# Four units with seven products in nearly every gate and up block of the two FFNs

## The chip, the core and the metric

The kernel runs on one core of a Trainium2 chip. Times are device microseconds (us) of one execution; "before" is the median of three runs. The profile is one further execution, taken by the hardware profiler, and its own time is given beside its span below. The engines are named as in the profile: PE (TensorE, matrix products), PEld (its weight loads), DVE (VectorE), ACT (ScalarE), POOL (GpSimd) and SP (whose queue issues most of the loads).

## The reference, cut to what matters

One decoder layer in float32: a SwiGLU half-step, a mixer with two gated linear recurrences, and a second SwiGLU half-step, each between two RMS norms. The change lies in the first two products of the two SwiGLU steps:

```python
def swiglu(x, w_gate, w_up, w_down):
    return (jax.nn.silu(x @ w_gate) * (x @ w_up)) @ w_down

f1 = swiglu(rms_norm(h, ffn1_pre_norm[l]), ffn1_w_gate[l], ffn1_w_up[l], ffn1_w_down[l])
h = h + 0.5 * rms_norm(f1, ffn1_post_norm[l])
# ... the mixer ...
f2 = swiglu(rms_norm(h, ffn2_pre_norm[l]), ffn2_w_gate[l], ffn2_w_up[l], ffn2_w_down[l])
```

`x` is 256 x 2048 and the gate and up weights are 2048 x 5504, so each weight is read once and used for two row tiles of 128.

## The kernel before

**Blocks.** Each FFN walks over the 5504 columns of gate and up in eleven blocks, `j = 0` to `10`: first a narrow one of 384 columns, then ten wide ones of 512. `gemm_pair` computes one block of gate and the same block of up together, for both row tiles: four sums, held in four PSUM tiles `c` (`c00`, `c01`, `c10`, `c11`: row tile, then gate or up). The inner dimension of 2048 is cut into eight units of 256. In the second FFN the narrow block goes through `gemm_block` instead, which is what `begin` being None stands for.

**A plain unit.** Every float32 number is split into two float32r parts, high and low, and a product is three matmuls: high by high (L159), low x by high w (L160), high x by low w (L161). ACT makes the high part `whi` of a weight tile (L153) and DVE the low part `wlo` by a subtraction (L155). A plain unit has two such 128x1024 chunks, one of gate and one of up, and eight products, which is 24 matmuls of 128x512.

**A unit with seven products.** `seven` does the same unit as a 2x2 block product by a scheme of the Strassen kind: sums of the four weight tiles are formed first, and then seven products are enough, which is 21 matmuls. DVE forms the sums (`wsum` 128x1024, `raw` 128x512, `wsum` 128x512, all at L245) and three low parts (two `wlo` of 128x1024 and `wsuml` of 128x1536, also L245). ACT makes four high parts (L280, L282, L284, L286), and the tiles arrive in four loads of 256 KB (L274 to L277) where a plain unit has two of 512 KB (L135). The low part `wsuml` comes last; its first reader on PE is the third matmul of the product `p5`, which is the first L161 matmul that reads `wsuml` in each such unit. The sums of `x` that these products need are made once per FFN (`operand_sums`).

**How many.** `SUMS` has three units with seven products (2, 4, 6), `FOUR` has four (2, 4, 5, 6). Where a block has four, the steps are set so that one plain chunk stands between two units with seven products:

```python
if late:
    at = range(6, 6 + 2 * len(sevens), 2)
elif len(sevens) > len(SUMS):
    at = range(3, 3 + 2 * len(sevens), 2)
else:
    at = [2 * u - j for j, u in enumerate(sevens)]
```

Before, blocks of odd `j` have four and wide blocks of even `j` three, in both FFNs. The last wide block is `j = 10`.

**The end of a block.** The first two chunks of the next block are split ahead (`following`). DVE adds the parts `psum` of the shared products (`share`), closes the four `c` tiles (L245, `c<-c,psum`), and multiplies by ACT's silu (L705). ACT then rearranges the two results (`halves`, L709), its queue issues two DMA transposes (L713), and some steps later it writes the turned rows to `hT` (L718). All of these stand in the in-order streams of DVE and ACT among the next block's splits.

**Buffers.** `raw`, `whi` and `wlo` have rings of five tiles, the row tiles (`wsum`, `wsumh`, `wsuml`, `psum`) a ring of three, and PSUM has eight tiles.

Of the kernel before, what the change touches and what calls it, by code (L numbers as in the profile page):

```python
# [33 lines left out]
SUMS = (2, 4, 6)  # L34
FOUR = (2, 4, 5, 6)
# [53 lines left out]
def kernel(ctx: ExitStack, tc: tile.TileContext, a: dict, out: bass.AP):  # L89
# [15 lines left out]
    def nm(s):  # L105
        uid[0] += 1
        return f"{s}_{uid[0]}"
# [55 lines left out]
    def gemm_block(w_dram, c0, w, lhs, nkt=KT, held=None, raws=(), ready=()):  # L163

        raws, ready = list(raws), list(ready)
        nb = -(-w // CB)
        step = 2 // nb  # L170
        pss = [[ps_tile(f"mm{t}") for _ in range(nb)] for t in range(NT)]

        def chunk(k0, alloc):
            if ready:
                return ready.pop(0)
            raw = raws.pop(0) if raws else None
            src = w_dram[k0 * P:(k0 + step) * P, c0:c0 + w]
            return wchunk(src.rearrange("(k p) c -> p k c", p=P) if nb == 1 else
                          src.rearrange("p (n c) -> p n c", n=nb), w // nb, alloc, raw)

        def mm(t, k0, parts):
            for i, part in enumerate(parts):
                kt = k0 + i % step
                mm3(pss[t][i // step][:, :w // nb], lhs(t, kt), part, kt == 0, kt == nkt - 1)

        if held is None:
            for k0 in range(0, nkt, step):
                parts = chunk(k0, ring_alloc)
                for t in range(NT):
                    mm(t, k0, parts)  # L190
                side.pump()
        else:
            kept = []
            for i, k0 in enumerate(range(0, nkt, 2)):
                kept.append((k0, chunk(k0, ring_alloc if i < RING else held)))
                mm(0, *kept[-1])
                side.pump()
            for k in kept:
                mm(1, *k)
                side.pump()  # L200
            side.flush()
        return pss if nb > 1 else [ps[0] for ps in pss]
# [122 lines left out]
    def first_of(w_dram, c0, w=CB):  # L325
        def chunk(i):
            return wchunk(w_dram[2 * i * P:2 * (i + 1) * P, c0:c0 + w]
                          .rearrange("(k p) c -> p k c", p=P), w)
        return chunk

    def gemm_pair(ws, w, lhs, sums, ready=(), following=(), raws=(), sevens=SUMS,
                  late=False):

        raws = list(raws)
        nu = KT // 2

        b = Blocks(lambda i, kt: ws[i][0][kt * P:(kt + 1) * P, ws[i][1]:ws[i][1] + w],  # L340
                   w, lhs, part_of(sums))

        def split(i, k0):
            return wchunk(None, w, raw=raws.pop(0)) if raws else first_of(*ws[i], w)(k0 // 2)

        steps = [(u, i) for u in range(nu) if u not in sevens for i in range(2)]
# [6 lines that stand above are left out]
        for j, u in zip(at, sevens):  # L355
            steps.insert(j, (u, None))
        ready = list(ready)
        for j, (u, i) in enumerate(steps):
            side.fast = late
            if any(i is None for _, i in steps[j:j + 2]):  # L360
                side.full = True
            if i is None:
                b.seven(u, u == sevens[-1])
                continue
            k0 = 2 * u
            parts = ready.pop(0) if ready else split(i, k0)
            if (u, i) == (nu - 1, 0) and sevens:
                ready = [split(1, k0)]
                b.share()
            for t in range(NT):  # L370
                b.plain((k0, k0 + 1), t, i, parts, u == nu - 1)
            side.pump()
        ready = [chunk(0) for chunk in following]
        for i in range(2 if sevens else 0):
            for t in range(NT):
                b.close(t, i)
        side.full = side.fast = False
        return *[[b.c[t][i] for t in range(NT)] for i in range(2)], ready
# [298 lines left out]
    def ffn(pre, x, rs, post, pre_next, begin=None, ready=(), then=None):  # L677
        with ExitStack() as fctx:
# [8 lines left out]
            def x_sums():  # L687
                return operand_sums(
                    x, lambda i: tiles4(new_part(i).rearrange("p i c -> p (i c)")), sums)

            raws = begin(x_sums) if begin else ()
# [9 lines left out]
            blocks = [FIRST] + list(range(0, FIRST, CB))  # L701

            def finish(t, f0, w, u, s):
# [13 lines left out]
                src = turned[:, :2 * n, :].rearrange("p (h j) k -> p h j k", h=2)  # L717
                nc.scalar.activation(dst.rearrange("p j (k h) -> p h j k", h=2), src, AF.Copy)  # L718

            for j, f0 in enumerate(blocks):  # L720
                w = min(CB, DFF - f0)
                following = [first_of(a[pre + s], f1) for f1 in blocks[j + 1:j + 2]
                             for s in ("_w_gate", "_w_up")]
                if j or begin:
                    g, u, ready = gemm_pair(
                        [(a[pre + "_w_gate"], f0), (a[pre + "_w_up"], f0)], w, xl, sums, ready,
                        following, () if j else raws, (FOUR if j % 2 else SUMS) if j else ())
                else:
                    g = gemm_block(a[pre + "_w_gate"], f0, w, xl, held=held, ready=ready)
                    ready = ()  # L730
                s = []
                for t in range(NT):
                    st = fwork.tile([P, CB], F32, tag="silu", name=nm("silu"))
                    nc.scalar.activation(st[:, :w], g[t][:, :w], AF.Silu, scale=rs[t])
                    s.append(st)
                if not (j or begin):
                    side.spawn(x_sums())
                    u = gemm_block(a[pre + "_w_up"], f0, w, xl)
                hT[f0 // CB] = fpool.tile([P, 4, NT * P], F32, tag="hT", name=nm("hT"), bufs=11)
                for t in range(NT):  # L740
                    side.spawn(finish(t, f0, w, u[t], s[t]))
# [537 lines left out]
    def begin(x_sums):  # L1279

        raws = []

        def load_h(*tns):
            for t, n in tns:
                nc.sync.dma_start(h[t][n], a["x"][t * P:(t + 1) * P, n * CB:(n + 1) * CB])

        def load_w(*ics):
            for i, c in ics:
                raws.append(wload(a[("ffn1_w_gate", "ffn1_w_up")[i]]
                                  [2 * c * P:2 * (c + 1) * P, FIRST:]  # L1290
                                  .rearrange("(k p) c -> p k c", p=P), DFF - FIRST,
                                  apart=not (i or c)))

        load_h((0, 0))
        load_w((0, 0))
        load_h((1, 0))
        load_w((1, 0), (0, 1))
        load_h((0, 1))
        load_w((1, 1))
        load_h((1, 1))  # L1300
        load_w((0, 2))
        load_h((0, 2), (1, 2), (0, 3), (1, 3))

        idle = work.tile([P, CB], F32R, tag="tmp", name="idle", bufs=3)
        nc.gpsimd.memset(idle.bitcast(F32), 0.0)
        ps = ps_tile()

        def idling(n):
            for _ in range(n):
                nc.tensor.matmul(ps, lhsT=idle[:, :P], rhs=idle, start=True, stop=True)  # L1310

        idling(9)
        tp = ps_tile()
        nc.tensor.transpose(tp[:, :KT], wrow, ident[:KT, :KT])
        first_ops.append(nc.vector.tensor_copy(wcol, tp[:, :KT]))
        side.spawn(first_norm(x, rs, idling, x_sums))
        return raws

    x, rs, ready = ffn("ffn1", x, rs, "ffn1_post_norm", wcols[:, 1, :], begin,
                       then=first_of(a["w_in"], O_GQ))  # L1320
    x, rs, ready = mixer(x, rs, ready, first_of(a["ffn2_w_gate"], FIRST, DFF - FIRST))
    ffn("ffn2", x, rs, "ffn2_post_norm", None, ready=ready)
    side.flush()

# [45 lines left out]
```

## Time and profile before

| | |
|---|---|
| median of 3 runs | 2064.32 us (2063.22 to 2066.75) |
| the profiled execution, its own time | 2066.25 us |
| its span in the profile | 2064.3 us |
| PE busy | 2051.2 us (99%) |
| DVE busy | 1858.0 us (90%) |
| ACT busy | 1304.9 us (63%) |

The span is what the profile shows from the first to the last instruction; the execution's own time is 1.95 us longer. Busy time counts an instruction from its start to its end, and consecutive instructions overlap a little on PE, DVE and ACT. In the rows of the timeline the first number is the start in us from the span's start, the second the duration (of all of them, where `x2` or more stand together), and a bracket gives the engine's idle time before the row and what ended it.

### The profile page before, as it was taken

What the parts mean: (1) busy time and instruction counts of PE and PEld (TensorE: products, weight loads), DVE (VectorE), ACT (ScalarE), POOL (GpSimd) and SP (SyncE); (2) the same over time, 40 slices, a digit from 0 to 9 for tenths busy, and PEclk for the clock granted to TensorE, in tenths of its full rate; (3) what the DMA queues carried; (4) which work ended last, traced back from release to release, by engine and by line L of the source; (5) the groups of instructions that cost most, each with busy time, mean ns of one, the idle gap of its engine ahead of it and who ended that gap; (6) DMA issues with size and microseconds to landing.
All of it is one profiled execution on the core that took longest, in us unless ns stands there. A gap on an engine that the chain in (4) does not pass through costs nothing. (4 is left out here: it accounts for less than half of the span.)

```text
span 2064.3 us, 28994 instructions
## 1 busy us (share of the span) xinstructions
PE 2051.2 (99%) x10337; PEld 1702.9 (82%) x10337; DVE 1858.0 (90%) x2187; ACT 1304.9 (63%) x1714; POOL 41.1 (2%) x87
## 2 busy tenths in 40 slices
PE   9999999999999999999999999999999999999998
PEld 9888888888888888878888888888888888888886
DVE  7999999998999779989999897578999999999996
ACT  7666666666666576577655554465666666766663
POOL 1000000000000100000000000010000000000000
PEclk9999999999999999999999999999999999999999
DMA  8767677676767467556565566747767767776663
GB/s 261 215 208 241 196 220 218 209 227 207 226 196 230 148 198 222 162 174 192 169 203 188 181 223 214 218 157 200 234 193 218 227 210 215 219 235 200 213 206 133
DMA packets 246105, 423.50 MB, mean 205 GB/s; under 512 B 63476, under 2 KB 71863, under 8 KB 245960
## 3 DMA queue, kind: packets, MB, share of 16 engines
q1 hardware_dynamic: 194896, 401.80, 61.7%
q10 hardware_dynamic: 51064, 19.84, 4.8%
q8 instruction: 81, 1.33, 0.3%
q14 instruction: 64, 0.52, 0.1%
HBM read 406.11 MB, written 4.19 MB: 199 GB/s over the span
## 5 line engine op out<-in xcount | busy, mean ns | idle before, releaser
L155 DVE TENSOR_TENSOR wlo<-raw,whi 128x1024 fp32r<-128x1024 f32 (+3 forms) x498 | 582.8, 1184 | 70.9 <-ACT whi L153 70.0
L153 ACT ACTIVATE whi<-raw 128x1024 fp32r<-128x1024 f32 (+3 forms) x498 | 504.8, 1026 | 217.5 <-PE c L160 74.0
L159 PE MATMUL c<-whi,xhi 128*128 128x512 f32 (+1 forms) x1270 | 494.5, 390 | 0.0
L161 PE MATMUL c<-wlo,xhi 128*128 128x512 f32 (+1 forms) x1270 | 491.5, 387 | 0.0
L160 PE MATMUL c<-whi,xlo 128*128 128x512 f32 (+1 forms) x1270 | 491.3, 387 | 0.0
L245 DVE TENSOR_TENSOR wlo<-raw,whi 128x1024 fp32r<-128x1024 f32 x252 | 299.4, 1218 | 36.9 <-ACT whi L284 23.6
L161 PEld LDWEIGHTS c<-wlo,xhi 128*128 128x128 f32 x1270 | 238.4, 188 | 47.9 <-DVE wlo L245 0.8
L159 PEld LDWEIGHTS c<-whi,xhi 128*128 128x128 f32 x1270 | 238.4, 188 | 47.4 <-ACT xhi L471 0.6
L160 PEld LDWEIGHTS c<-whi,xlo 128*128 128x128 f32 x1270 | 238.5, 188 | 46.2
L284 ACT ACTIVATE whi<-raw 128x1024 fp32r<-128x1024 f32 x126 | 133.1, 1057 | 201.2 <-DVE raw L245 95.0
L245 DVE TENSOR_TENSOR wsuml<-wsum,wsumh 128x1536 fp32r<-128x1536 f32 x126 | 220.6, 1751 | 8.0 <-ACT wsumh L286 8.0
L160 PE MATMUL c<-whi,hklo 128*128 128x512 f32 x558 | 217.2, 389 | 0.3 <-DVE hklo L155 0.3
L161 PE MATMUL c<-wlo,hkhi 128*128 128x512 f32 x558 | 217.2, 389 | 0.1
L159 PE MATMUL c<-whi,hkhi 128*128 128x512 f32 x558 | 217.2, 389 | 0.0
L282 ACT ACTIVATE wsumh<-wsum 128x1024 fp32r<-128x1024 f32 x126 | 132.6, 1053 | 92.7 <-DVE wsum L245 70.7
L280 ACT ACTIVATE whi<-raw 128x1024 fp32r<-128x1024 f32 x126 | 132.4, 1051 | 60.8 <-PE c L160 49.4
L245 DVE TENSOR_TENSOR wsum<-raw,raw 128x1024 f32<-128x1024 f32 x126 | 153.4, 1218 | 18.2 <-DMA raw<-in_ffn_w_down_dram 15.7
L160 PEld LDWEIGHTS c<-whi,hklo 128*128 128x128 f32 x558 | 104.7, 188 | 22.3 <-DVE hklo L155 0.6
L161 PEld LDWEIGHTS c<-wlo,hkhi 128*128 128x128 f32 x558 | 104.7, 188 | 22.2 <-DVE wlo L245 0.5
L159 PEld LDWEIGHTS c<-whi,hkhi 128*128 128x128 f32 x558 | 104.7, 188 | 21.8
L245 DVE TENSOR_TENSOR c<-c,psum 128x512 f32<-128x512 f32 x135 | 87.4, 690 | 11.5 <-PE c L161 11.2
L245 DVE TENSOR_TENSOR wsum<-raw 128x512 f32<-128x512 f32 x126 | 87.0, 690 | 3.6
(346 smaller groups left out, 3153.4 us busy)
## 6 DMA issues: line engine op xcount, KB each, us to landing
raw<-in_ffn_w_down_dram SPq DMA_DIRECT2D x124, 512.0 KB, 4.7
raw<-in_w_in_dram SPq DMA_DIRECT2D x104, 512.0 KB, 4.5
raw<-in_ffn_w_gate_dram SPq DMA_DIRECT2D x90, 512.0 KB, 4.6
raw<-in_ffn_w_up_dram SPq DMA_DIRECT2D x90, 512.0 KB, 4.4
raw<-in_ffn_w_gate_dram SPq DMA_DIRECT2D x140, 256.0 KB, 4.0
raw<-in_ffn_w_up_dram SPq DMA_DIRECT2D x140, 256.0 KB, 3.9
raw<-in_w_in_dram SPq DMA_DIRECT2D x128, 256.0 KB, 3.6
raw<-in_ffn_w_down_dram SPq DMA_DIRECT2D x96, 256.0 KB, 3.7
```

What stands on the lines that cost most here:

```text
L153: last[0] = nc.scalar.activation(hi, src, AF.Copy)
L155: nc.vector.tensor_tensor(lo, src, hi.bitcast(F32), op=ALU.subtract)
L159: nc.tensor.matmul(ps, lhsT=xhi, rhs=whi, start=start, stop=False)
L160: nc.tensor.matmul(ps, lhsT=xlo, rhs=whi, start=False, stop=False)
L161: nc.tensor.matmul(ps, lhsT=xhi, rhs=wlo, start=False, stop=stop)
L245: return nc.vector.tensor_tensor(o, x, y, op=op)
L280: nc.scalar.activation(ahi, ra, AF.Copy)
L282: nc.scalar.activation(hi[:, 0:2, :], wsum[:, 0:2, :], AF.Copy)
L284: nc.scalar.activation(bhi, rb, AF.Copy)
```

## The change

A new function chooses the units of a block. In the first FFN `begin` is set, and blocks 1 to 9 have four units with seven products. In the second FFN blocks 2 to 9 have four, and block 1 has three. Block 10 keeps three in both.

```diff
+            def sevens_of(j):
+                if not j:
+                    return ()
+                return FOUR if j < len(blocks) - 1 and (begin or j > 1) else SUMS
+
             for j, f0 in enumerate(blocks):
...
                 if j or begin:
                     g, u, ready = gemm_pair(
                         [(a[pre + "_w_gate"], f0), (a[pre + "_w_up"], f0)], w, xl, sums, ready,
-                        following, () if j else raws, (FOUR if j % 2 else SUMS) if j else ())
+                        following, () if j else raws, sevens_of(j))
```

So blocks 2, 4, 6 and 8 of each FFN go from three such units to four, and block 1 of the second FFN from four to three: seven units more in all, and 21 matmuls fewer.

The order of instructions moves at the seams between blocks. DVE in the first FFN, from the last multiplication by silu of block 3 to the first `wsuml` of block 4, before (block 4 has three units; the first two rows are the two plain chunks that come ahead of its first unit with seven products):

```order
L705 SCALAR_TENSOR_TENSOR silu_1659<-c_265_1312,r_421,silu_1659 128x512
L155 TENSOR_TENSOR wlo_1703<-raw_1700,whi_1702 128x1024
L155 TENSOR_TENSOR wlo_1721<-raw_1718,whi_1720 128x1024
L245 TENSOR_TENSOR wsum_1738<-raw_1736,raw_1737 128x1024
L245 TENSOR_TENSOR raw_1737<-wsum_1738,raw_1736 128x512
L245 TENSOR_TENSOR wsum_1738<-raw_1737 128x512
L245 TENSOR_TENSOR wlo_1746<-raw_1736,whi_1745 128x1024
L245 TENSOR_TENSOR wlo_1748<-raw_1737,whi_1747 128x1024
L245 TENSOR_TENSOR wsuml_1740<-wsum_1738,wsumh_1739 128x1536
```

And DVE at such a seam now (blocks 4 and 5 of the first FFN, both with four units):

```order
L705 SCALAR_TENSOR_TENSOR silu_2022<-c_345_1675,r_421,silu_2022 128x512
L155 TENSOR_TENSOR wlo_2066<-raw_2063,whi_2065 128x1024
L245 TENSOR_TENSOR wsum_2083<-raw_2081,raw_2082 128x1024
L245 TENSOR_TENSOR raw_2082<-wsum_2083,raw_2081 128x512
L245 TENSOR_TENSOR wsum_2083<-raw_2082 128x512
L245 TENSOR_TENSOR wlo_2091<-raw_2081,whi_2090 128x1024
L245 TENSOR_TENSOR wlo_2093<-raw_2082,whi_2092 128x1024
L245 TENSOR_TENSOR wsuml_2085<-wsum_2083,wsumh_2084 128x1536
```

One plain `wlo` stands between the silu and the unit's second `wlo` (`wlo_2093`) where two stood. That second `wlo` needs `whi_2092`, which ACT makes behind the transposes; ACT at the same seam now:

```order
L709 ACTIVATE halves_2043<-silu_2020 128x1024
L709 ACTIVATE halves_2047<-silu_2022 128x1024
L713 DMA_TRANSPOSE turned_2045<-halves_2043 128x8x128
L713 DMA_TRANSPOSE turned_2049<-halves_2047 128x8x128
L282 ACTIVATE wsumh_2084<-wsum_2083 128x1024
L284 ACTIVATE whi_2092<-raw_2082 128x1024
L286 ACTIVATE wsumh_2084<-wsum_2083 128x512
```

ACT's order here is the one it had before between blocks 3 and 4; only DVE's order moved. The seam between blocks 1 and 2 of the first FFN is the exception: there the plain `wlo` stands ahead of the last close, and DVE now has none between the silu and the unit:

```order
L245 TENSOR_TENSOR c_110_596<-c_110_596,psum_910 128x512
L705 SCALAR_TENSOR_TENSOR silu_955<-c_108_594,r_414,silu_955 128x512
L705 SCALAR_TENSOR_TENSOR silu_957<-c_110_596,r_421,silu_957 128x512
L245 TENSOR_TENSOR wsum_1018<-raw_1016,raw_1017 128x1024
L245 TENSOR_TENSOR raw_1017<-wsum_1018,raw_1016 128x512
```

Before, one plain `wlo` stood between `silu_957` and that `wsum`.

## The prediction

> **What bounds the kernel now.** I read the page first, then the gate and up stage in four windows, then DVE and PE row by row over one pair of blocks, since both look nearly full.
>
> ```profile
> PE 2051.2 (99%) x10337; PEld 1702.9 (82%) x10337; DVE 1858.0 (90%) x2187; ACT 1304.9 (63%) x1714; POOL 41.1 (2%) x87
> ```
>
> ```profile
> 1540.30:1580.90 40.60, 40.60 (x181) 33.61 (x180) 38.65 (x40) 26.76 (x29) 0.00 (x0) 1.00 0.80 242
> 1580.90:1622.60 41.70, 41.70 (x186) 34.53 (x185) 39.56 (x41) 28.07 (x32) 0.00 (x0) 1.00 0.65 193
> ```
>
> The first is the page's line of busy times, the others are two windows (length, then PE, PEld, DVE, ACT, POOL, clock, DMA): a block with three units with seven products, then one with four. PE is full in both; DVE lacks 2 us of being full. How much lead DVE has on PE, and whether four such units fit under PE, is read from the rows. PE, the first matmul that reads `wsuml`, in four consecutive such units:
>
> ```profile
> 1575.67 0.39 PE L161 MATMUL p<-wsuml,hkhi 128*128 128x512 f32 x1
> ...
> 1594.03 0.39 PE L161 MATMUL p<-wsuml,hkhi 128*128 128x512 f32 x1
> ...
> 1601.51 0.39 PE L161 MATMUL p<-wsuml,hkhi 128*128 128x512 f32 x1
> ...
> 1608.99 0.39 PE L161 MATMUL p<-wsuml,hkhi 128*128 128x512 f32 x1
> ```
>
> Inside a block of four these lie 7.48 us apart, which is 33 matmuls (21 of the unit, 12 of the plain chunk between), so 0.2267 us each. From the last such unit of a block to the first of a block of four lie five plain chunks and a unit, 81 matmuls, 18.36 us. PE thus needs 3 x 7.48 + 18.36 = 40.80 us for a block of four, and 0.68 more for a block of three. DVE beside it:
>
> ```profile
> 1590.38 1.75 DVE L245 TENSOR_TENSOR wsuml<-wsum,wsumh 128x1536 fp32r<-128x1536 f32 x1
> ...
> 1598.04 1.75 DVE L245 TENSOR_TENSOR wsuml<-wsum,wsumh 128x1536 fp32r<-128x1536 f32 x1
> 1599.71 1.22 DVE L155 TENSOR_TENSOR wlo<-raw,whi 128x1024 fp32r<-128x1024 f32 x1
> ...
> 1603.43 2.35 DVE L245 TENSOR_TENSOR wlo<-raw,whi 128x1024 fp32r<-128x1024 f32 x2
> 1605.70 1.75 DVE L245 TENSOR_TENSOR wsuml<-wsum,wsumh 128x1536 fp32r<-128x1536 f32 x1
> ...
> 1613.37 1.75 DVE L245 TENSOR_TENSOR wsuml<-wsum,wsumh 128x1536 fp32r<-128x1536 f32 x1
> ...
> 1632.75 1.75 DVE L245 TENSOR_TENSOR wsuml<-wsum,wsumh 128x1536 fp32r<-128x1536 f32 x1
> ```
>
> DVE's `wsuml` come every 7.66 us, with no idle bracket on a row: DVE is 0.18 us slower than PE in each step of the dense stretch. The first `wsuml` ends at 1590.38 + 1.75 = 1592.13, 1.90 us before PE reads it; after three steps 1.90 - 3 x 0.18 = 1.36 are left. From the last unit of this block to the first of the next, which has three, DVE takes 19.38 us without idling, for six plain chunks and all closing work. PE needs 18.36 + 2.72 (12 matmuls) = 21.08 there, so the lead grows by 1.70. It is the block of three that refills DVE's lead, and the change takes it away.
>
> **The change, part by part.** PE loses 21 matmuls in all: 21 x 0.2267 = 4.76 us, if nothing takes PE's place.
>
> *DVE in a changed block.* A plain unit costs it two chunks, each 2.35 - 1.22 = 1.13 us from start to start; a unit with seven products costs 7.66 - 1.13 = 6.53. Each exchange adds 6.53 - 2.27 = 4.26 us; seven make 30 us. Between two blocks of four the seam has five plain chunks where it had six: 19.38 - 1.13 = 18.25 us of work, against PE's 18.36. That would nearly fit, but at such a seam DVE also waits for ACT. The trace of before holds the same DVE order once, in the second FFN between blocks 1 and 2:
>
> ```profile
> 1460.90 1.40 DVE L705 SCALAR_TENSOR_TENSOR silu<-c,r,silu 128x512 f32<-128x512 f32 x2
> 1462.22 1.21 DVE L155 TENSOR_TENSOR wlo<-raw,whi 128x1024 fp32r<-128x1024 f32 x1
> ...
> 1465.94 1.22 DVE L245 TENSOR_TENSOR wlo<-raw,whi 128x1024 fp32r<-128x1024 f32 x1
> 1467.68 1.23 DVE L245 TENSOR_TENSOR wlo<-raw,whi 128x1024 fp32r<-128x1024 f32 x1 [0.53 <-ACT whi L284]
> ```
>
> ```profile
> 1461.68 2.00 ACT L709 ACTIVATE halves<-silu 128x1024 uint16<-128x1024 uint16 x2 [0.21 <-DVE silu L705]
> 1462.77 2.83 ACTq L713 DMA_TRANSPOSE turned<-halves  x2
> 1465.64 1.06 ACT L282 ACTIVATE wsumh<-wsum 128x1024 fp32r<-128x1024 f32 x1 [1.96 <-DVE raw L245]
> 1466.61 1.04 ACT L284 ACTIVATE whi<-raw 128x1024 fp32r<-128x1024 f32 x1
> ```
>
> The chain is DVE's silu, ACT's two `halves`, 2.83 us in which ACT's queue issues two transposes and computes nothing, then L282 and L284, and only then DVE's second `wlo`. All of it hangs on DVE's own silu, so more lead or less does not change it. The two `wlo` start 1.74 us apart instead of 1.13: 0.61 us lost per seam. So DVE needs 3 x 7.66 + 18.25 + 0.61 = 41.84 us for a block of four behind a block of four, 1.04 more than PE and 0.36 more than PE's block of three (41.48). Once the lead is gone, each block ends at DVE's pace.
>
> The Trainium skill ("DMA: Bandwidth & Descriptors", section "Issuing engines are not separate DMA queues") says that the time a sequencer takes to initiate a DMA is usually small relative to the DMA itself. The row of the transposes disagrees for this seam; by the rule the 0.61 would be nothing, and the time would be that of the first rival below.
>
> *First FFN.* These rows start and end the stretch:
>
> ```profile
> 75.17 1.75 DVE L245 TENSOR_TENSOR wsuml<-wsum,wsumh 128x1536 fp32r<-128x1536 f32 x1
> ...
> 78.36 0.39 PE L161 MATMUL p<-wsuml,hkhi 128*128 128x512 f32 x1
> ...
> 95.16 1.75 DVE L245 TENSOR_TENSOR wsuml<-wsum,wsumh 128x1536 fp32r<-128x1536 f32 x1
> ...
> 404.38 0.69 DVE L155 TENSOR_TENSOR hklo<-hT,hkhi 128x512 fp32r<-128x512 f32 x1
> 404.99 1.22 DVE L245 TENSOR_TENSOR wlo<-raw,whi 128x1024 fp32r<-128x1024 f32 x1
> 406.12 1.75 DVE L245 TENSOR_TENSOR wsuml<-wsum,wsumh 128x1536 fp32r<-128x1536 f32 x1
> ...
> 407.92 0.50 PE L161 MATMUL p<-wsuml,hkhi 128*128 128x512 f32 x1
> ```
>
> Block 1 ends with a lead of 78.36 - 76.92 = 1.44 us. Block 2's first `wsuml` starts at 95.16, before and now: the plain chunk that now is missing was covered by the same ACT chain, so DVE only idles 1.13 longer. PE wants it at 78.36 + 18.36 = 96.72, and it ends at 96.91: PE waits from here on. Block 9's first `wsuml` starts at 95.16 + 7 x 41.84 = 388.04, its last at + 22.98 + 0.61 (the `hklo` that stands in this block before and now) = 411.63; it ends at 413.38, and PE reads it 0.05 later (as 407.92 stands to 406.12 + 1.75). 413.43 against 407.92: +5.5 us. From there nothing differs, and before, too, the lead at this row was nought.
>
> *Second FFN.* Block 1 now has three, and PE gets there what it lost to waits:
>
> ```profile
> 1427.26 0.39 PE L161 MATMUL p<-wsuml,hkhi 128*128 128x512 f32 x1
> ...
> 1435.62 0.50 PE L161 MATMUL p<-wsuml,hkhi 128*128 128x512 f32 x1 [0.72 <-DVE wsuml L245]
> ...
> 1451.78 0.50 PE L161 MATMUL p<-wsuml,hkhi 128*128 128x512 f32 x1
> ...
> 1781.44 0.50 PE L161 MATMUL p<-wsuml,hkhi 128*128 128x512 f32 x1
> ```
>
> Its first unit comes one chunk later, 1427.26 + 2.72 = 1429.98; the others follow with two chunks between, 45 matmuls or 10.20 us each: 1440.18 and 1450.38, 1.40 earlier than 1451.78. I take no wait for them, as DVE has 4.26 us less to do. Block 2 starts with the lead of 1.90 that a block of four has behind a block of three: PE at 1468.74, DVE's end at 1466.84. Its last ends 22.98 later, block 9's 7 x 41.84 = 292.88 after that, plus 0.61: 1783.31, and PE at 1783.36 against 1781.44: +1.9 us.
>
> *Tails.* Where DVE has no lead, whatever delays ACT at a seam counts in full. Two such delays stand in the trace, at 345.18 and at 1749.93:
>
> ```profile
> 334.90 2.73 ACTq L713 DMA_TRANSPOSE turned<-halves  x2
> ...
> 345.18 1.37 ACT L718 ACTIVATE hT<-turned 128x1024 uint16<-128x1024 uint16 x1 [2.58 <-DMA turned<-halves]
> ...
> 1591.52 2.58 ACT L718 ACTIVATE hT<-turned 128x1024 uint16<-128x1024 uint16 x2
> ...
> 1749.93 2.39 ACTq L713 DMA_TRANSPOSE turned<-halves  x1
> ```
>
> Their effect is already in 407.92 and 1781.44; for new ones I add 0.5 us, an estimate: two in some twenty seams, about 1 us each (2.39 against half of the pair's 2.73; 1.5 for the other, below), and a part of them is in those numbers already.
>
> *What costs nothing.* ACT gains 1.6 us of work per exchange at 63% load. SP issues two loads more per exchange, 14 in all; no row of the dense stretch of four waits for a load, and a block of four behind another repeats that stretch. If this cover were gone, DVE's first `wsum` would wait. The nearest row is a wait list's, from the down product:
>
> ```profile
> DVE wsum L245 <- DMA raw<-in_ffn_w_down_dram: 15.7, 8, 3.1
> ```
>
> That is 2.0 us each (15.7 in 8 waits, the longest 3.1). So the price lies between 0 and 2.0 us per seam, and not below, as no load is dropped; I take 0, nearest to the rows of the same stage.
>
> The sum: 5.5 + 1.9 + 0.5 = +7.9 us. The profiled execution took 2066.25, so 2074.1 in its terms; it lies 1.9 over the median of the runs, and against that median of 2064.32 the forecast is 2072.
>
> **The rivals.**
>
> *The seam's wait is hidden* (if ACT gets L284 out earlier than the rows above show). DVE then needs 41.23 per block: the first FFN comes to 5.5 - 1.74 - 7 x 0.61 = -0.5, the second to 1.9 - 7 x 0.61 = -2.4, in all 2061.5. Against it speaks that ACT's order at the seam is the same as in the rows.
>
> *The lead lasts* and PE keeps its pace, which ends on the faster side. It decides if DVE's cycle falls under 40.80, that is if the 0.18 per step and the seam's wait both vanish. PE alone would reach block 9's row at 78.36 + 8 x 40.80 = 404.76 (-3.2) and 1468.74 + 22.44 + 7 x 40.80 = 1776.78 (-4.7): 2056.5. For it speaks DVE's 90% on the page; against it the even drift in every row of the dense stretch.
>
> *The transposes land late at the seams*, and ACT's wait at L718 holds the next unit. Now ACT reaches the second L718 about 5.6 us after the transposes are issued (six operations, 1 us each), and I find 0.4 us of room behind it. The one of 345.18 landed 7.55 us after (the issue ended at 334.90 + 2.73), so it would cost 1.5. At every one of 15 seams that is +22 us; at every third +7.5, or 2079. Against it: at the blocks of four before, as in the row of 1591.52, L718 waited for nothing.
>
> **How the numbers follow.** The forecast gets 0.62, with its own range 2068 to 2076 (0.61 per seam down to 0.35, or two tails more). The hidden wait gets 0.13, the lasting lead 0.05, late transposes 0.14, and 0.06 stays for what I do not see. The range 2063 to 2079 leaves out the lasting lead, most of the hidden wait and the worst of the late transposes, about 0.2. A change of 0.2% (4.1 us) is about what the measurement can tell. Faster by that: the lasting lead and a bit of the hidden wait, 0.08. Within it, 2060.2 to 2068.4: the rest of the hidden wait and the forecast's low end, 0.18. Slower: 0.74.
>
> **What would show it.** Right: `wsuml` reads on PE carry waits for DVE from block 2 on in the first FFN and from about block 4 in the second; blocks 3 to 9 last 41.8 us each; at each seam DVE's second `wlo` waits some 0.5 us for L284; the second FFN's block 1 has no waits. Wrong: blocks of 40.8 us (the lead lasts) or of 41.2 (no wait at the seam), or L718 rows with waits for `turned` at most seams.

## The result, and the profile after

The changed kernel takes 2079.48 us (median of 4 runs, 2078.92 to 2080.75), the kernel before beside it 2065.30 (4 runs): ratio 1.0068, 95% interval 1.0056 to 1.008, or +14.2 us where +7.9 was forecast. The profiled execution has a span of 2079.0 us, 14.7 over that of before, and an own time of 2080.75.

PE does 21 matmuls less and is busy 8 us longer by the page's first lines. A matmul that waits for its weights, or that runs at a lower clock, has a longer record (0.50 to 0.68 us in rows below instead of 0.39), and so PE counts as busy:

```profile
PE 2059.4 (99%) x10316; PEld 1693.5 (81%) x10316; DVE 1886.4 (91%) x2215; ACT 1318.1 (63%) x1728; POOL 41.1 (2%) x87
```

Two blocks of four behind a block of four, in the second FFN (length, then PE, PEld, DVE, ACT, POOL, clock, DMA):

```profile
1546.80:1588.65 41.85, 41.85 (x185) 34.02 (x184) 41.05 (x42) 28.18 (x31) 0.00 (x0) 1.00 0.71 212
1588.65:1630.50 41.85, 41.85 (x184) 33.66 (x183) 41.05 (x42) 28.10 (x31) 0.00 (x0) 1.00 0.71 215
```

Both last 41.85 us, as forecast (41.84). The seam at which the second one starts, first DVE's rows, then ACT's (start, duration, idle time ahead and what ended it):

```profile
1595.37 1.22 DVE L245 TENSOR_TENSOR wlo<-raw,whi 128x1024 fp32r<-128x1024 f32 x1
1597.11 1.23 DVE L245 TENSOR_TENSOR wlo<-raw,whi 128x1024 fp32r<-128x1024 f32 x1 [0.52 <-ACT whi L284]
```

```profile
1592.19 2.83 ACTq L713 DMA_TRANSPOSE turned<-halves  x2
1595.06 1.07 ACT L282 ACTIVATE wsumh<-wsum 128x1024 fp32r<-128x1024 f32 x1 [1.96 <-DVE raw L245]
1596.03 1.04 ACT L284 ACTIVATE whi<-raw 128x1024 fp32r<-128x1024 f32 x1
...
1599.39 2.57 ACT L718 ACTIVATE hT<-turned 128x1024 uint16<-128x1024 uint16 x2
```

The second `wlo` again starts 1.74 us after the first, because its `whi` stands behind the two transposes on ACT. The `hT` rows carry no wait: the transposes have landed in time here. That the place behind the transposes is the cause is tested below.

Where, then, are the other microseconds? The list of waits (total, times, longest) of after, and of before:

```profile
DVE held L155 <- ACT held L153: 17.2, 7, 7.5
ACT hT L718 <- DMA turned<-halves: 16.7, 8, 5.9
...
PEld p L161 <- DVE wlo L245: 15.4, 32, 1.9
```

```profile
ACT hT L718 <- DMA turned<-halves: 12.4, 10, 4.2
...
DVE held L155 <- ACT held L153: 3.9, 6, 1.0
...
PEld p L161 <- DVE wlo L245: 1.3, 3, 0.9
```

Two things grew: PE's waits for DVE, most of which stand at the pace of the blocks, and DVE's waits for `held`. `held` is the high part of a sum of `hT`, which the down product's units with seven products need. Its longest wait lies at the end of the second FFN's gate and up stage, behind block 10. ACT there after, then before:

```profile
1840.94 2.84 ACTq L713 DMA_TRANSPOSE turned<-halves  x2
1843.88 1.06 ACT L153 ACTIVATE whi<-raw 128x1024 fp32r<-128x1024 f32 x1 [2.02 <-PE c L161]
1846.67 1.38 ACT L718 ACTIVATE hT<-turned 128x1024 uint16<-128x1024 uint16 x1 [1.73 <-DMA turned<-halves]
1853.95 1.34 ACT L718 ACTIVATE hT<-turned 128x1024 uint16<-128x1024 uint16 x1 [5.90 <-DMA turned<-halves]
1855.17 0.60 ACT L153 ACTIVATE held<-sums 128x512 fp32r<-128x512 f32 x1
```

```profile
1834.23 2.80 ACTq L713 DMA_TRANSPOSE turned<-halves  x2
1837.08 0.63 ACT L153 ACTIVATE held<-sums 128x512 fp32r<-128x512 f32 x1 [1.93 <-DVE wsum L245]
...
1838.56 1.35 ACT L718 ACTIVATE hT<-turned 128x1024 uint16<-128x1024 uint16 x1
1840.58 1.37 ACT L718 ACTIVATE hT<-turned 128x1024 uint16<-128x1024 uint16 x1 [0.67 <-DMA turned<-halves]
```

Two things differ. Before, `held` stands ahead of both `hT` rows; after, behind them. And the second transpose lands late: from the end of its issue (1840.94 + 2.84 = 1843.78) to its `hT` row it takes 10.2 us, where it took 3.6. (This is what landing after so many us means below.) DVE and PE beside it, after:

```profile
1847.66 0.69 DVE L155 TENSOR_TENSOR hklo<-hT,hkhi 128x512 fp32r<-128x512 f32 x1
1855.80 0.69 DVE L155 TENSOR_TENSOR held<-sums,held 128x512 fp32r<-128x512 f32 x1 [7.46 <-ACT held L153]
```

```profile
1853.99 0.39 PE L161 MATMUL c<-wlo,hkhi 128*128 128x512 f32 x1
1856.77 0.68 PE L159 MATMUL p<-whi,hkhi 128*128 128x512 f32 x1 [2.39 <-ACT whi L280]
...
1859.02 0.79 PE L161 MATMUL p<-wlo,hkhi 128*128 128x512 f32 x1 [1.14 <-DVE wlo L245]
1859.61 0.63 PE L159 MATMUL c<-whi,held 128*128 128x512 f32 x1
1860.03 0.63 PE L160 MATMUL c<-whi,held 128*128 128x512 f32 x1
```

DVE stands still for 7.5 us, and PE runs out of split weights and waits twice. The longer wait, 2.39 us, is for ACT itself: L280 stands behind both `hT` rows (before, too), so it comes late with the second of them. The next, 1.14 us, is for DVE's `wlo`. Then PE waits no more, but ten matmuls start 0.43 us apart instead of 0.23. The granted clock (the column behind POOL's) is at half here. In the second execution of the same kernel (last experiments) it is not, with the same two waits ahead of it (1.39 and 1.51 us):

```profile
1857.00:1863.70 6.70, 5.56 (x13) 3.88 (x13) 6.67 (x8) 6.01 (x8) 0.00 (x0) 0.50 0.69 214
```

```profile
1857.00:1863.70 6.70, 4.25 (x17) 3.09 (x18) 6.67 (x7) 6.70 (x9) 0.00 (x0) 1.00 0.45 148
```

The ten slow matmuls are some 2 us (10 x 0.20); whether they add to what an end costs is taken up with the two runs.

What runs beside the transposes is on SP's queue; its issues after, then before:

```profile
1841.67 0.33 SPq L276 DMA_DIRECT2D raw<-in_ffn_w_down_dram  x1
1842.05 0.43 SPq L277 DMA_DIRECT2D raw<-in_ffn_w_down_dram  x1
1842.82 3.74 SPq L135 DMA_DIRECT2D raw<-in_ffn_w_down_dram  x3
```

```profile
1831.87 8.66 SPq L135 DMA_DIRECT2D raw<-in_ffn_w_down_dram  x3
```

After, five loads (two of 256 KB, three of 512 KB) go out within 5.3 us of the first transpose's issue. Before, the three rows on one line start at 1831.87, 1835.5 and 1840.2, so one load goes out 1.3 us after it and the next 6.0 us after it.

To see which rows repeat, both kernels were run a second time (last two experiments). PE's reads of `wsuml` that the prediction used as marks, after (last of the first FFN's block 9, first of the second FFN, last of its block 9):

```profile
413.38 0.39 PE L161 MATMUL p<-wsuml,hkhi 128*128 128x512 f32 x1
...
1436.47 0.39 PE L161 MATMUL p<-wsuml,hkhi 128*128 128x512 f32 x1
...
1791.20 0.39 PE L161 MATMUL p<-wsuml,hkhi 128*128 128x512 f32 x1
```

The second FFN's first unit stands one plain chunk (2.72 us) later by the change itself, so its mark is taken less 2.72. Differences of marks, us, the two executions of each kernel:

| stretch | before | after | difference of means | forecast |
|---|---|---|---|---|
| start to block 9, first FFN | 407.9, 408.3 | 413.4, 412.7 | +4.9 | +5.5 |
| from there to the second FFN's first unit | 1019.3, 1017.1 | 1020.4, 1023.8 | +3.9 | 0 |
| from there to its block 9 | 354.2, 354.4 | 357.4, 356.5 | +2.7 | +1.9 and 0.5 of tails |
| from there to the end | 282.9, 284.7 | 287.8, 287.6 | +3.9 | 0 |

The blocks cost 7.6 us, about as forecast (7.9 with the tails). The two ends of the stages cost 7.7 on the mean, where nothing was forecast; the first of them differs from run to run (2.2 and 5.6). The spans of these executions differ by 15.4 on the mean, a little more than the medians.

### The profile page after: what moved, and what is told of

Its sections match the earlier page's. It is cut to its first block, busy times and chain, and to the rows that moved or that the text cites. A ratio compares the mean times of both kernels' runs of the same rounds, so it can differ in the third digit from the quotient of the medians.

```text
span 2079.0 us, 28942 instructions
## 1 busy us (share of the span) xinstructions
PE 2059.4 (99%) x10316; PEld 1693.5 (81%) x10316; DVE 1886.4 (91%) x2215; ACT 1318.1 (63%) x1728; POOL 41.1 (2%) x87
## 5 line engine op out<-in xcount | busy, mean ns | idle before, releaser
L153 ACT ACTIVATE whi<-raw 128x1024 fp32r<-128x1024 f32 (+3 forms) x484 | 489.3, 1025 | 215.0 <-PE c L160 56.1
L155 DVE TENSOR_TENSOR wlo<-raw,whi 128x1024 fp32r<-128x1024 f32 (+3 forms) x484 | 567.2, 1184 | 62.2 <-ACT whi L153 61.4
L159 PE MATMUL c<-whi,xhi 128*128 128x512 f32 (+1 forms) x1221 | 476.9, 391 | 0.0
L160 PE MATMUL c<-whi,xlo 128*128 128x512 f32 (+1 forms) x1221 | 472.7, 387 | 0.0
L161 PE MATMUL c<-wlo,xhi 128*128 128x512 f32 (+1 forms) x1221 | 469.5, 388 | 0.0
L245 DVE TENSOR_TENSOR wlo<-raw,whi 128x1024 fp32r<-128x1024 f32 x266 | 316.2, 1219 | 19.8 <-ACT whi L284 16.3
L161 PEld LDWEIGHTS c<-wlo,xhi 128*128 128x128 f32 x1221 | 229.1, 188 | 51.8 <-DVE wlo L245 3.6
L159 PEld LDWEIGHTS c<-whi,xhi 128*128 128x128 f32 x1221 | 229.2, 188 | 49.5 <-ACT whi L284 4.9
L245 DVE TENSOR_TENSOR wsuml<-wsum,wsumh 128x1536 fp32r<-128x1536 f32 x133 | 233.1, 1752 | 7.4 <-ACT wsumh L286 7.4
L284 ACT ACTIVATE whi<-raw 128x1024 fp32r<-128x1024 f32 x133 | 139.7, 1050 | 86.1 <-DVE raw L245 48.0
L280 ACT ACTIVATE whi<-raw 128x1024 fp32r<-128x1024 f32 x133 | 139.7, 1051 | 57.0 <-PE c L160 26.7
```

What stands on the lines that cost most here:

```text
L153: last[0] = nc.scalar.activation(hi, src, AF.Copy)
L155: nc.vector.tensor_tensor(lo, src, hi.bitcast(F32), op=ALU.subtract)
L159: nc.tensor.matmul(ps, lhsT=xhi, rhs=whi, start=start, stop=False)
L160: nc.tensor.matmul(ps, lhsT=xlo, rhs=whi, start=False, stop=False)
L161: nc.tensor.matmul(ps, lhsT=xhi, rhs=wlo, start=False, stop=stop)
L245: return nc.vector.tensor_tensor(o, x, y, op=op)
```

## The experiments

Theory A in the expectations: the blocks go at DVE's pace, and the ends cost because block 10's transposes land late. The rivals differ from run to run.

**One FFN at a time.** First FFN as after, second as before:

```diff
-                return FOUR if j < len(blocks) - 1 and (begin or j > 1) else SUMS
+                if not begin:
+                    return FOUR if j % 2 else SUMS
+                return FOUR if j < len(blocks) - 1 else SUMS
```

> First FFN as in the changed kernel, second FFN as before. Theory A (DVE's pace of 41.84 us per block of four, and a separate cost at the end of each FFN because the last block's transposes land late): block 9's last wsuml of the first FFN is read on PE at about 413.4 instead of 407.9 (+5.5), +1.0 more by the end of this FFN, then the rows of before, all shifted: about +6.5 us, or 2071.8 against 2065.3. Rival B (the pace alone, with nothing at the end of an FFN): +5.5, or 2070.8. Rival C (the cost at the end of the second FFN comes from something that the first FFN leaves behind, not from the second FFN's own order): the stretch from block 9's row of the second FFN to the end is long here too, 287.8 instead of 282.9 us, and the time is about 2076.7.

And the reverse (`if begin: return FOUR if j % 2 else SUMS`, else as after):

> Second FFN as in the changed kernel, first FFN as before. Theory A: block 9's row of the second FFN comes 1.9 us later than before (3 if block 2 again starts with less lead than 1.90), and the stretch from that row to the end takes 287.8 instead of 282.9 us since the second transpose of block 10 lands 10 us after its issue: +6.8 to +8, or about 2072.5. Together with the run in which only the first FFN is changed it makes up the whole +14.2. Rival B (the cost at the end is an accident of the one profiled execution): +1.9 to +3, or 2067.7. Rival C (the first FFN causes it): the same as B, 2067.7.

Measured: 2072.31 against 2065.01 (ratio 1.0037, 1.0025 to 1.005), so +7.3; and 2070.85 (1.0032, 1.0019 to 1.0044), so +5.8. They add up to 13.1 of the 14.2. The stretch from the second FFN's block 9 to the end takes 282.7 us in the first kernel and 288.1 in the second, so this end belongs to the second FFN's own blocks (rival C of both falls), and it is no accident of one execution (rival B of the second falls). For the first FFN's end the runs of the first kernel decide less: they lie between 2068.1 and 2075.6, and in the profiled one, the shortest of them, the stretch behind block 9 cost nothing (1017.8 us, with a landing after 6.6). Theory A's +6.5 and rival B's +5.5 are both within the interval. DVE's wait for `held` in the two kernels:

```profile
DVE held L155 <- ACT held L153: 7.3, 6, 4.3
```

```profile
DVE held L155 <- ACT held L153: 11.0, 6, 7.1
```

**Three units in block 8.** This puts a block of three ahead of the last pair:

```diff
-                return FOUR if j < len(blocks) - 1 and (begin or j > 1) else SUMS
+                return FOUR if j not in (8, 10) and (begin or j > 1) else SUMS
```

> As the changed kernel, but block 8 of both FFNs has three units with seven products, so that DVE has lead again when block 9 starts, and block 10's instructions at its end stand in the order of before. Theory A: block 9's row of the first FFN at about +3.7 us, of the second at about +0.3 beside the first's shift; the last block's transposes land within 4 us of their issue and the ends of both FFNs cost nothing: about +4.0, or 2069.3, although PE has 42 matmuls (9.5 us) more than in the changed kernel's two blocks. Rival B (the end's cost has nothing to do with the lead or order at block 10): the 5.9 us at the ends stay, about 2075.

Measured: 2069.31 (1.0024, 1.0015 to 1.0034), +4.3, where theory A had +4.0. PE has 6 matmuls (1.4 us) more than in the changed kernel, not the 42 that the expectation says, and the kernel is still 10 us nearer to before. The second transpose of block 10 lands 4.3 and 4.7 us after its issue in the two FFNs. In the second FFN, DVE's lead at block 10's three units is about that of the changed kernel (0.67, 0.60 and 1.52 us against 0.78, 0.37 and 1.29; in the first FFN it is longer, 1.91, 1.62 and 2.54 against 0.91, 0.10 and 1.13). So it is not the lead by itself but the order at block 10's end, with `held` ahead of `hT` again, that goes with the early landing. Not all of theory A came true in the profiled execution, which was the slowest of the ten: the first FFN's end cost nothing, but from the second FFN's block 9 to the end it took 286.0 us, 2.2 more than the mean of before, without a late landing. What these 2.2 are stays open (before itself spreads over 1.9).

**Three units in block 9.**

```diff
-                return FOUR if j < len(blocks) - 1 and (begin or j > 1) else SUMS
+                return FOUR if j < len(blocks) - 2 and (begin or j > 1) else SUMS
```

> As the changed kernel, but block 9 of both FFNs has three units too, so that block 10 comes behind a block of three with a refilled lead, and the order of its end is yet another one. Theory A (the lead or order at block 10 sets when the loads meet the transposes): the second transpose lands within 5 us, and the stretch from the end of block 9 to the end costs nothing; blocks 2 to 8 still last 41.84 us: -0.7 to -1.2 us for the seams and rows saved, and about -6 for the two ends: 2072. Rival B (a kernel with the dense blocks has late transposes whatever stands in block 9): 2079.

Measured: 2069.91 against 2065.41 (1.0024, 1.0015 to 1.0033). The changed kernel, run beside it on the same chip, took 2080.89: one unit with seven products less per FFN makes it 11 us faster. ACT at the second FFN's end:

```profile
1838.28 0.63 ACT L153 ACTIVATE held<-sums 128x512 fp32r<-128x512 f32 x1 [1.84 <-DVE wsum L245]
...
1841.77 1.37 ACT L718 ACTIVATE hT<-turned 128x1024 uint16<-128x1024 uint16 x1 [0.65 <-DMA turned<-halves]
```

`held` is ahead again, the landing takes 3.5 us, and the stretch to the end 283.3 us. Theory A holds, rival B falls.

**The loads taken away.** The changed kernel, and the kernel before, without six loads of the down product per FFN:

```diff
         def split(hf, kt, alloc=ring_alloc):
+            if not hf and 8 <= kt < 14:
+                t = ring.tile([P, RW], F32, tag="raw", name=nm("raw"))[:, :2 * CB].rearrange(
+                    "p (i c) -> p i c", i=2)
+                nc.gpsimd.memset(t, 0.0)
+                return wchunk(None, CB, alloc, (t, False))
```

> As the changed kernel, but the six plain chunks 8 to 13 of the down product's first half are not loaded in either FFN: their tiles are set to zero by POOL, so these twelve loads and the right values are left out. Theory A (block 10's second transpose lands 10 to 12 us after its issue because weight loads run beside it): it lands within 5 us, ACT's second hT row waits for nothing or at most 1 us, the PE gaps behind it go, and the stretch from block 9's row of the second FFN to the end takes about 283 us instead of 287.8; time about 2072. Rival B (the transposes are slow by themselves at this place): landing and stretch stay as in the changed kernel, 2079. Rival C (the transposes land early, but the stretch stays at 287 to 288 since the order of block 10's end on ACT and DVE costs it, not the landing): 2078.

> The kernel before with the same twelve loads left out: what these loads cost by themselves. Theory A: in the kernel before the second transpose landed 5 us after its issue and ACT waited 0.7 us for it, so the loads cost it little: stretch of 282 to 283 us, time 2063 to 2065. Rival (the loads delay the start of the down product in any order): 3 us or more faster than the kernel before.

These two kernels leave out loads and so part of the result. Measured: the changed kernel without them 2069.48 against 2064.66 (1.0024, 1.0014 to 1.0034), +4.8 where the changed kernel had +14.2; the kernel before 2061.97 against 2064.66 (0.9989, 0.998 to 0.9998), 2.7 us less. So without these loads the change costs 7.5 us, about what the blocks cost, and 6.7 of its 14.2 go with the loads, a little less than the two ends cost (7.7). ACT at the second FFN's end, the changed kernel without the loads (the added lines shift L713 and L718 by five):

```profile
1836.44 2.84 ACTq L718 DMA_TRANSPOSE turned<-halves  x2
...
1841.76 2.60 ACT L723 ACTIVATE hT<-turned 128x1024 uint16<-128x1024 uint16 x2 [1.31 <-DMA turned<-halves]
1844.23 0.60 ACT L153 ACTIVATE held<-sums 128x512 fp32r<-128x512 f32 x1
```

The order is that of the changed kernel, `held` behind `hT`. But the second transpose is there 3.7 us after its issue, the second `hT` row follows the first without a wait, DVE waits 1.4 us for `held` instead of 7.5, and the stretch to the end takes 281.3 us. Theory A holds; its rivals B and C fall, since neither the transposes alone nor the order alone costs the time. In the kernel before, whose transposes landed early anyway, the same loads cost 2.7 us, close to the 3 of the rival there. That they delay the down product a little in any order fits this, but is not shown by a row.

**The transposes behind the next unit.** For the pace of the blocks: ACT issues the transposes, and later `hT`, behind the first unit of the next block.

```diff
-                nc.scalar.dma_start_transpose(turned[:, :2 * n, :], halves[:, :2 * w])
-                for _ in range(6):
+                for _ in range(3):
+                    yield
+                with tc.issue_after(last[0].ins):
+                    nc.scalar.dma_start_transpose(turned[:, :2 * n, :], halves[:, :2 * w])
+                for _ in range(3):
                     yield
...
-                nc.scalar.activation(dst.rearrange("p j (k h) -> p h j k", h=2), src, AF.Copy)
+                with tc.issue_after(last[0].ins):
+                    nc.scalar.activation(dst.rearrange("p j (k h) -> p h j k", h=2), src, AF.Copy)
```

> As the changed kernel, but the two transposes of a block (and later the two hT rows) are issued by ACT behind the first unit of the next block, so that they no longer stand ahead of the two high parts (L282, L284) that this unit's second wlo waits for. Theory A (the wait of 0.61 us of DVE for L284 at each seam makes a block of four last 41.84 us): blocks of four behind four last 41.23 us, the first unit of block 2 in the first FFN comes 1.13 us earlier, and the time falls by 15 x 0.61 + 1.13 = about 10 us, to 2069.5, with the ends of the FFNs as in the changed kernel if block 10's transposes land as late as there. Rival B (the order on DVE itself, or another wait, sets the 41.84): no change, 2079.5.

Measured: 2068.42 against 2064.66 (1.0018, 1.0009 to 1.0027), +3.8 where the changed kernel had +14.2, so 10.4 us less. The windows of two blocks of four, DVE's two `wlo` at the seam between them, and ACT's rows there:

```profile
1579.90:1621.25 41.35, 41.35 (x182) 33.51 (x181) 41.06 (x42) 28.37 (x31) 0.00 (x0) 1.00 0.74 216
1621.25:1662.60 41.35, 41.35 (x184) 34.22 (x184) 41.06 (x42) 28.33 (x32) 0.00 (x0) 1.00 0.71 214
```

```profile
1627.96 2.35 DVE L245 TENSOR_TENSOR wlo<-raw,whi 128x1024 fp32r<-128x1024 f32 x2
```

```profile
1627.65 1.04 ACT L284 ACTIVATE whi<-raw 128x1024 fp32r<-128x1024 f32 x1
1628.08 1.25 ACTq L716 DMA_TRANSPOSE turned<-halves  x1
```

L284 now comes ahead of the transposes, the two `wlo` follow each other without a wait, and the block lasts 41.35 us instead of 41.85 (41.23 was expected). Theory A holds. Block 10's end keeps the changed kernel's order here, and the transposes land late as there (7.5 and 9.2 us after the issue); from the second FFN's block 9 to the end it takes 287.9 us, as in the changed kernel. Pace and end are two costs.

**Block 1 of the second FFN alone.** The kernel before with three units there (`FOUR if j % 2 and (begin or j > 1) else SUMS`):

> The kernel before, but block 1 of the second FFN has three units instead of four. Theory: PE gets back the waits of this block (1451.78 against 1450.38, 1.40 us) and block 2 onwards keeps it: -1.4 us, or 2063.9. Rival (DVE and the transposes at the seams set the end of the stretch anyway, and 21 matmuls more are 4.76 us): same or slower, up to +3, 2068.

Measured: 2064.51 against 2065.01 (1.0001, 0.9992 to 1.001). The interval holds both -1.4 us and no change, so this part is not settled by the time. (PE has 3 matmuls more here, 0.68 us, not the 21 of the expectation.) The profiled execution has block 9's row 4.8 us earlier than before, and the stretch behind it 1.9 us longer.

**Two versions meant to be faster**, both with the transposes behind the next unit, and with blocks of three where DVE's lead runs out:

```diff
-                return FOUR if j < len(blocks) - 1 and (begin or j > 1) else SUMS
+                return SUMS if j in ((5, 10) if begin else (1, 6, 10)) else FOUR
```

> A version meant to be faster than both: transposes behind the next block's first unit, four units with seven products in blocks 1 to 4 and 6 to 9 of the first FFN (three in 5 and 10) and in 2 to 5 and 7 to 9 of the second (three in 1, 6 and 10). Theory A: with DVE's cycle at 41.23 us the lead of 1.9 us falls by 0.43 per block of four and is refilled by the block of three, so PE keeps 40.80 us per block of four: five exchanges more of 0.68 us against the kernel before in all (-3.4) and up to -1.4 for block 1 of the second FFN: 2060 to 2062. Rival B (the lead does not hold, because PE waits behind the seams): 2065 or more.

```diff
-                return FOUR if j < len(blocks) - 1 and (begin or j > 1) else SUMS
+                return SUMS if j in ((4, 8, 10) if begin else (1, 5, 8, 10)) else FOUR
```

> A more careful form of the mixed version: transposes behind the next block's first unit; in the first FFN blocks 4, 8 and 10 have three units and the others four, in the second FFN 1, 5, 8 and 10 have three. Theory: a block of three after every three of four refills DVE's lead before it is used up, the last block starts with lead as in the kernel before, and its transposes land within 4 to 5 us. Three exchanges more than before (-2.0 us) and the first wide block of the second FFN (-0.5 as measured for it alone, up to -1.4): 2061 to 2062.5. Rival (the lead was not what held the mixed version; the rest is chance from run to run): 2063.9, as the first mixed version.

Measured: the first 2063.89 against 2064.66 (0.9991, 0.9982 to 1.0), between theory and rival; its single runs lie between 2060.0 and 2065.8, and what spreads them stays open. The second 2059.29 (7 runs, 2058.17 to 2059.69) against 2065.41: ratio 0.9972, 0.9961 to 0.9983, or -6.1 us, faster than both kernels of this case and by 1.7 us or more faster than expected; its rival (2063.9) falls. Two of PEld's entries for DVE in its list of waits, then the larger of the two in that of before:

```profile
PEld p L161 <- DVE wsuml L245: 2.1, 7, 0.4
...
PEld p L161 <- DVE wlo L245: 0.4, 2, 0.2
```

```profile
PEld p L161 <- DVE wsuml L245: 5.9, 11, 1.1
```

Three exchanges more than before are 9 matmuls, 2.0 us. The other 4 us would be waits: these two entries come to 2.5 us here and to 7.2 in the list of before (5.9 and the 1.3 shown above). No run takes the two parts apart. The last block's transposes land after 4.2 and 3.7 us.

**The two kernels once more.**

> The changed kernel once more, to see which rows of one execution repeat. If the late landing belongs to this order: block 10's second transpose lands 8 us (first FFN) and 10 us (second) after its issue again, and the second FFN's stretch from block 9's row to the end takes about 287.8 us again; time 2079. If it was chance: 283 us in this execution.

> The kernel before once more. If the rows of the kernel before repeat: block 9's row of the first FFN at 407.9, the second FFN from its first unit to block 9's row 354.2 us, from there to the end 282.9, landing of block 10's second transpose 3.5 to 4.4 us after its issue. The second of these was 351.9 in the run with only the first FFN changed, so 352 to 354 is expected if single seams differ by chance.

Measured: 2080.89 for the changed kernel (1.0076, 1.0062 to 1.009), 2066.27 for the kernel before (1.0004, 0.9994 to 1.0013). The late landing repeats (11.7 and 9.2 us), and so do the early ones (4.3 and 5.1 us); the marks are in the table above. Over all runs with all loads: in the eight ends of FFNs where `held` stands behind `hT` and five loads go out within 5.3 us of the transposes, the second one lands 6.6 to 11.7 us after its issue and DVE waits 4.3 to 8.6 us for `held`. In the fifteen where `held` stands ahead and one load goes out in that time, it lands 3.5 to 5.1 us after, and DVE waits 0.2 us at most. One end, the first FFN's in the first mixed version, lies between: `held` behind `hT`, three loads, landing after 4.3 us, and a wait of 2.0. What an end costs follows the landing: against the mean of the kernel before, the first FFN's end cost -0.4, +0.6, +2.2 and +5.6 us with landings after 6.6 (first FFN changed alone), 7.5 (transposes behind the unit), 8.1 and 11.7 us (the changed kernel, twice). At the second FFN's four landings after 9.2 to 10.2 us cost 3.8 to 4.3. By these eight, a landing after up to some 7 us was free, and what came on top of that was paid.

The clock stands beside this. In four of the eight ends with a late landing it was granted at half, for 3.4 or 6.8 us, and in no end with an early one. In the first FFN these are just the two dear ends (2.2 and 5.6 us, with 3.4 and 6.8 us of half clock; 8 or 9 slow matmuls are at most some 1.8 us each time), so there the clock may have a part in the cost. In the second FFN the cost does not follow it: 3.9, 3.8, 4.3 and 4.1 us with 6.8, 0, 3.4 and 0 us at half. So the waits behind a late landing are enough by themselves for this cost.

## Why the prediction was right and wrong

**Right: the pace.** A block of four behind a block of four was put at 41.84 us, at DVE's pace; 41.85 was measured. Block 9's mark of the first FFN was put at 413.43 and stood at 413.38 and 412.68. The seam's wait is shown as the cause by the run that moves the transposes: 0.50 us per block go, where 0.61 was forecast. The rivals of the hidden wait (2061.5) and of the lasting lead (2056.5) are out.

The rule of the Trainium skill weighed in the prediction ("DMA: Bandwidth & Descriptors", section "Issuing engines are not separate DMA queues": the time it takes to initiate a DMA is usually small relative to the DMA itself) does not carry here. The two transposes take 2.83 us of ACT's queue to issue, and in the run that moves them behind L284 the block is 0.50 us shorter.

**Right in size, with another split: the second FFN.** Forecast 1.9 for its blocks and 0.5 for tails, measured +2.7. The lead of 1.90 at block 2, which the prediction took over from other seams, was there when only this FFN was changed, and its blocks cost 2.2 us there. In the changed kernel it was not: the two transposes ahead of that unit took 3.5 us to issue and the lead was 0.7 in the first execution, 2.7 and 1.5 in the second. That the sum came out so near is in part luck.

**Wrong: "From there nothing differs."** This step priced everything behind block 9 at nothing, and it cost 3.9 us at each FFN's end on the mean, 7.7 in all. Block 10 has three units in both kernels, so its own code is the same, but behind blocks 8 and 9 of four units its instructions stand in another order: `held` behind `hT` instead of ahead of it, and the down product's loads closer behind the transposes. With three units in block 8 or in block 9 both are as before. Beside these loads the second transpose lands late, and the in-order ACT queue turns that into a stop of DVE, and into a late `whi` (L280) for which PE waits. That order was there to be read before any run; the prediction looked at the seams of the dense stretch and not at the last one.

**Half right: the rival of late transposes.** Its mechanism, ACT held at L718 by a transpose that lands late, is what cost the missing time, and its 2079 for "every third seam" happens to be the time measured. But it was placed at the seams between blocks of four, where no `hT` row of the changed kernel waited longer than 0.7 us. It came at the two ends, with landings after 8 to 12 us, and that the two numbers meet is luck. The range's upper end took that 2079 and left out the worse cases of this rival.

**What stays open.** Whether `held` behind `hT` alone, with the loads as far apart as before, would cost anything: no run has that order with those loads. DVE then would wait for `hT` in any case; in the run without the loads it waited 1.25 and 1.40 us. The reverse, a late landing with `held` ahead, is in no run either; L280 stands behind both `hT` rows in either order. Open is also what part of the first FFN's end belongs to the half clock.

## What to carry to other kernels

A seam that is repeated is priced well from rows; a seam that happens once, where one stage hands over to the next, has to be read in the new order by itself, even where its own code is unchanged. Look there for an operation that another engine waits for and that now stands behind a wait for a DMA in an in-order queue. And where DVE and PE are both nearly full, a denser unit pays only as often as the lead it uses up is refilled: four in nearly every block cost 14 us; with a block of three after at most three of four, and the transposes out of the way, they gained 6.

## What the runs showed of the hardware

How late a small DMA lands depends on what is in flight beside it, far more than expected. The second of the same two transposes of 128x1024 landed 3.5 to 5.1 us after its issue with one to three weight loads beside it, and 6.6 to 11.7 us after it with five. The run without six of the loads shows that they are the cause (3.7 us instead of 10.2, in the same order). The queues' totals in the changed kernel (packets, MB, share of 16 engines; q1 holds SP's loads, q10 ACT's transfers):

```profile
q1 hardware_dynamic: 195120, 401.80, 61.6%
q10 hardware_dynamic: 51064, 19.84, 4.7%
```

By these, a packet of the loads has 2.1 KB on the mean, one of ACT's queue 0.4 KB. The Trainium skill ("DMA: Bandwidth & Descriptors", section "Queues, rings and completion order") says that a DMA engine takes turns between the queues that it has work for, one packet each (a packet there holds several descriptors; whether the profile's packets are the same unit, no run shows). By that rule a queue of small packets gets the smaller share of the bytes while loads are in flight, which agrees with the late landings; no run here tests the rule by itself. It would not explain all: while the late transpose of the second FFN was in flight, the DMA engines together moved less than the mean of the span (204 GB/s), although they count as busy (length, then the engines, clock, DMA share, GB/s):

```profile
1848.00:1850.00 2.00, 2.00 (x11) 1.65 (x10) 0.34 (x1) 0.05 (x1) 0.00 (x0) 1.00 1.39 133
```

So more than the sharing of bytes slows them there; what it is stays open.

The granted TensorE clock can fall within a kernel that keeps PE busy for 99% of its span. In the fourteen executions of these experiments it was at half, apart from the first and last 8 us of each span, only at ends of FFNs at which PE had waited over 1 us for its weights, for 3.4 or 6.8 us, and matmuls then started 0.43 us apart instead of 0.23. Of seven such ends four had it and three had not, so such a wait alone does not decide it.
